# A streaming trunk's first norm: x in a second layout, squares summed by ScalarE's accumulator, the scale spread by a matmul

## The chip, the cores and the metric

The kernel runs on one core of a Trainium2 chip. The metric is the time of one execution on the device in microseconds (us). Before the change, three runs gave a median of 1671.03 us (1669.79 to 1671.99).

The engines of the core are called PE (TensorE, matrix products), ACT (ScalarE), DVE (VectorE), POOL (GpSimd) and SP (SyncE, which here only issues DMAs). PEld is PE's loading of stationary operands.

## The reference, cut to what matters

One layer of a trunk on x with 256 tokens and 2048 channels, all in float32. In short:

```python
h = rmsnorm(x, g1)                       # x * rsqrt(mean(x*x, channels) + 1e-6) * g1
xa, ya, cb, cc, cx, ga, gb = split(h @ w_in + b_in, 7)      # each 2048 wide
a = rg_lru(causal_conv4(xa) + bias)      # gates from lru_wr, lru_wi; a scan over tokens
out_a = (a * gelu(ya)) @ w_pa
out_b = (cb * causal_conv3(cc * cx)) @ w_pb
x = x + (sigmoid(ga) * out_a + sigmoid(gb) * out_b) @ w_o
x = x + relu(rmsnorm(x, g2) @ w_mlp1) ** 2 @ w_mlp2
out = rmsnorm(x, final_g)
```

## The kernel before, in words

All activations lie transposed: channels on the 128 partitions, tokens along the row. x is a tile of 128 x 16 x 256 (channel block k, token). A product takes weight blocks of 128 x 128 as the stationary operand and 256 tokens as the moving one.

To keep float32 accuracy on a faster matmul format, every operand is split into a high and a low part: ACT casts it to float32r (the high part, L51 for weights, L122 and L126 for activations), and DVE subtracts that from the original (the low part, L52, L123, L127). A block then takes two matmuls: L236 (L265 in the first four products) multiplies the high weight with both parts of the activation, 512 columns, and L237 (L266) the low weight with the high part, 256 columns. The two halves of the PSUM tile are added when it is evicted: `added` copies the second half to SBUF on ACT (L242) and adds the first on DVE (L244).

Weights come as slabs of 512 KB, eight blocks each (class `Weights`). A slab is loaded by SP (L59) into one of four raw buffers, then split into one of four buffers each for high and low parts. `take` asks for slabs up to three ahead of the one used (LOOK). The splits carry a higher priority than what stands around them in the program.

The first norm is folded: the products run on x * g1 without the scale rsqrt(mean + eps), and each evicted column block of `h @ w_in` is multiplied with the scale `rs` (L249) before the bias and the function are applied (L250). `rs` is a tile of 128 x 256, the same row on each partition. So the first products can start before the scale is known.

The start of the kernel, in the order in which the program is written:

1. Nine matmuls on a tile of ones (L161).
2. Eight times: a load of two channel blocks of x (256 KB, L164), the loads of w_in for those blocks (two of 256 KB, L179) and the splits.
3. Three slabs ahead (L185), then the rest of the parameters (L186; the first 16 columns came at L166).
4. `first_four`: four products of w_in at once, two of xa and two of ya, block by block as they land (L265, L266). They hold four PSUM buffers of the pool `psz`, which has six.
5. `first_norm`: eight squares on ACT (L274, 512 columns each), seven adds on DVE that fold them to two (L278), two matmuls with ones that sum over the partitions (L143), and `rsqrt`: square root on ACT (L150), then four arithmetic operations on DVE and a reciprocal, 256 columns each (L152 to L156).
6. Eight groups g of two column blocks. Group 0 begins with the evictions of the first four products (L293 and L301, through `z_done`), then runs the products cb, cc and cx; `decay` (L203, small operations on 128 x 16) stands in group 0 too. Then come the gates, the scan and the splits of the results.

Behind this come the merge, the output product, the two MLP stages and the final norm, none of which the diff touches.

The framework takes the program and writes one fixed list of instructions for each engine, and adds the semaphore waits that the data need. An engine's list is not always the order of the program: an instruction with a higher priority, or one whose inputs are expected earlier, can stand ahead. On the chip each engine works through its list in order and waits where an instruction's inputs or buffers are not there.

Of the kernel before, what the change touches and what calls it, by code (L numbers as in the profile page):

```python
# [9 lines left out]
F32 = mybir.dt.float32  # L10
F32R = mybir.dt.float32r
AF = mybir.ActivationFunctionType
ALU = mybir.AluOpType
# [12 lines left out]
WAKE = 9  # L26

PARAMS = [("g1", NT), ("g2", NT), ("gf", NT), ("b_in", 7 * NT), ("ca_w", 4 * NT), ("ca_b", NT),
          ("br", NT), ("bi", NT), ("lam", NT), ("cb_w", 3 * NT), ("one", 1)]
OFF = {}  # L30
_n = 0
for _name, _w in PARAMS:
# [40 lines left out]


@with_exitstack
def trunk(ctx: ExitStack, tc: tile.TileContext, xT, par, w_in, w_lru, w_pa, w_pb, w_o, w_1, w_2, out):
    nc = tc.nc
    big = ctx.enter_context(tc.tile_pool(name="big", bufs=3))
    keep = ctx.enter_context(tc.tile_pool(name="keep", bufs=1))
# [37 lines left out]
    def pc(name, j):  # L117
        return pr[:, OFF[name] + j:OFF[name] + j + 1]
# [55 lines left out]
    for i in range(NT // 2):  # L174
        load_x(2 * i, 2)
        c, o = divmod(i, HALF // 2)
        raw = rawp.tile([P, 4, 2 * P], F32, name="raw")
        for q, z in enumerate((Z_XA, Z_YA)):
            nc.sync.dma_start(raw[:, 2 * q:2 * q + 2, :],  # L179
                              w_in[z:z + 2, c, :, o * 2 * P:(o + 1) * 2 * P].rearrange("m p n -> p m n"))  # L180
            if i == 0:
                W.split(fhi[:, i, 2 * q:2 * q + 2], flo[:, i, 2 * q:2 * q + 2], raw[:, 2 * q:2 * q + 2])
        if i:
            W.split(fhi[:, i], flo[:, i], raw)
    W.ahead(LOOK)  # L185
    nc.sync.dma_start(pr[:, NT:], par[:, NT:])  # L186

    def squares(src, j):

# [57 lines left out]
    def z_done(ps, j, dst, func):  # L247
        t = added(ps)
        nc.vector.tensor_tensor(t, t, rs, ALU.mult)  # L249
        nc.scalar.activation(dst, t, func, bias=pc("b_in", j))  # L250

    def z_product():
        return product(lambda k: xg[:, k], 0, 2)

    def z_tile(j, dst, func):
        z_done(z_product(), j, dst, func)
# [11 lines left out]

    early = first_four()

    def first_norm(pool):
        parts = [pool.tile([P, 2, S], F32, name=n) for n in ("xc", "gy", "cb", "cc", "gate0", "gate1", "q", "v")]
        for k in range(HALF):
            nc.scalar.activation(parts[k], x[:, 2 * k:2 * k + 2, :], AF.Square, scale=pc("one", 0))  # L274
        n = HALF // 2
        while n:
            for k in range(n):
                nc.vector.tensor_tensor(parts[k], parts[k], parts[n + k], ALU.add)  # L278
            n //= 2
        rsqrt(rs, [parts[0][:, 0, :], parts[0][:, 1, :]])  # L280

    ua = big.tile([P, NT, 2, S], F32R, name="big")
    ub = big.tile([P, NT, 2, S], F32R, name="big")
    with tc.tile_pool(name="w1", bufs=1) as w1:
        first_norm(w1)
        for g in range(NB):
            xa = w1.tile([P, 2, S + 3], F32, name="xa")
            xc = w1.tile([P, 2, S], F32, name="xc")
# [1 line left out]
            for m in range(2):  # L290
                j = 2 * g + m
                nc.gpsimd.memset(xa[:, m, 0:3], 0.0)
                z_done(early[m] if g == 0 else z_product(), Z_XA + j, xa[:, m, 3:], AF.Identity)  # L293
                c = xc[:, m, :]
                nc.vector.tensor_scalar(c, xa[:, m, 3:], pc("ca_w", 3 * NT + j), pc("ca_b", j), ALU.mult, ALU.add)
                for tap in (2, 1, 0):
                    nc.vector.scalar_tensor_tensor(c, xa[:, m, tap:tap + S], pc("ca_w", tap * NT + j), c, ALU.mult, ALU.add)  # L297
                split(xs[:, m], c)
            gy = w1.tile([P, 2, S], F32, name="gy")
            for m in range(2):  # L300
                z_done(early[2 + m] if g == 0 else z_product(), Z_YA + 2 * g + m, gy[:, m, :], AF.Gelu_apprx_tanh)  # L301
            cb = w1.tile([P, 2, S], F32, name="cb")
            cc = w1.tile([P, 2, S], F32, name="cc")
            cx = w1.tile([P, 2, S + 2], F32, name="cx")
# [147 lines left out]
```

## Time and profile before

| | |
|---|---|
| median of three runs | 1671.03 us |
| time of the profiled execution | 1670.37 us |
| its span, first to last instruction | 1668.5 us |
| PE busy | 1648.3 us, 99% |
| DVE busy | 1124.8 us, 67% |
| ACT busy | 866.2 us, 52% |
| mean granted clock of PE | 0.996 |

The profile is of one execution. Times in timelines count from the span's start. Busy time of PE is modelled from pipelined matmuls, so consecutive matmuls overlap in the rows: the pace is read from the distance of their starts. The granted clock is a share of full speed. "idle before <-X" says how long the engine was idle before an instruction, and which instruction's end released it.

### The profile page before, as it was taken

The numbers are of one execution on the slowest core, as the hardware profiler recorded it, in microseconds if no ns is written. First come the engines' busy times: TensorE is split into PE (matmuls) and PEld (weight loads), VectorE is DVE, ScalarE is ACT, GpSimd is POOL, SyncE is SP. The second block draws the span as 40 slices with busy tenths as digits, with TensorE's granted clock in tenths as the row PEclk, the third lists the DMA queues.
The fourth block names the chain that finished last, engine by engine and source line by source line (L and its number), as shares of the span: only waits on it lengthen the run. The fifth ranks groups of instructions, "written<-read, shape, count | busy, mean of one in ns | idle before, by whom it ended". The sixth has DMA issues, their size and how long they took to land.

```text
span 1668.5 us, 24306 instructions
## 1 busy us (share of the span) xinstructions
PE 1648.3 (99%) x9468; PEld 1440.4 (86%) x9468; DVE 1124.8 (67%) x1606; ACT 866.2 (52%) x1259; POOL 3.4 (0%) x37
## 2 busy tenths in 40 slices
PE   9899999999999999999999999999999999999996
PEld 8788888888888888888888888888888888888886
DVE  6889778878977565666666766665555666655554
ACT  7666656666665444444455544444443444444442
POOL 0000000000000000000000000000000000000000
PEclk9999999999999999999999999999999999999998
DMA  8455555555556555555555555555555555555552
GB/s 282 152 190 189 190 187 187 183 190 189 188 181 196 189 186 187 188 188 189 190 189 184 183 190 189 188 189 187 187 187 188 188 189 189 189 189 188 188 186 96
DMA packets 89715, 312.14 MB, mean 187 GB/s; under 512 B 9856, under 2 KB 14336, under 8 KB 89600
## 3 DMA queue, kind: packets, MB, share of 16 engines
q1 hardware_dynamic: 89312, 309.93, 56.2%
q8 instruction: 74, 1.21, 0.3%
q10 hardware_dynamic: 288, 0.66, 0.1%
q14 instruction: 41, 0.34, 0.1%
HBM read 308.45 MB, written 2.10 MB: 186 GB/s over the span
## 4 chain that ended last, share of the span: by engine, by line
PE 98%; DVE 1%; DMA 0%; ACT 0%; issue 0%; DVEq 0%; SPq 0%
PE psz L236 63%; PE psz L237 32%; PE psz L265 1%; PE psz L266 0%; PE psl L330 0%; PE psl L331 0%; PE psl L329 0%; DVE wlo L52 0%; PE psz L233 0%; PE psz L234 0%; PE psz L232 0%; DVE x L406 0%; DMA raw<-w_in_s 0%; DVE t L153 0%; DVE v L351 0%
## 5 line engine op out<-in xcount | busy, mean ns | idle before, releaser
L236 PE MATMUL psz<-big,whi 128*128 128x512 f32 x4016 | 1409.5, 394 | 4.8 <-DVE t L244 4.6
L237 PE MATMUL psz<-big,wlo 128*128 128x256 f32 x4016 | 1121.5, 279 | 0.0
L52 DVE TENSOR_TENSOR wlo<-raw,whi 128x1024 fp32r<-128x1024 f32 x576 | 703.6, 1224 | 509.0 <-ACT whi L51 507.8
L51 ACT CAST whi<-raw 128x1024 fp32r<-128x1024 f32 x576 | 604.5, 1049 | 767.4 <-issue 432.2
L236 PEld LDWEIGHTS psz<-big,whi 128*128 128x128 f32 x4016 | 753.3, 188 | 185.1 <-issue 4.9
L237 PEld LDWEIGHTS psz<-big,wlo 128*128 128x128 f32 x4016 | 753.3, 188 | 0.0
L236 PE MATMUL psz<-mg,whi 128*128 128x512 f32 x496 | 174.6, 395 | 0.0
L237 PE MATMUL psz<-mg,wlo 128*128 128x256 f32 x496 | 139.0, 281 | 0.0
L236 PEld LDWEIGHTS psz<-mg,whi 128*128 128x128 f32 x496 | 93.0, 187 | 22.1 <-DVE mg L123 0.3
L244 DVE TENSOR_TENSOR t<-psz,low 128x256 f32<-128x256 f32 x255 | 105.9, 418 | 0.0
L242 ACT COPY low<-psz 128x256 f32<-128x256 f32 x255 | 93.1, 365 | 3.1 <-DVE t L244 2.7
L237 PEld LDWEIGHTS psz<-mg,wlo 128*128 128x128 f32 x496 | 93.7, 189 | 0.0
L249 DVE TENSOR_TENSOR t<-t,rs 128x256 f32<-128x256 f32 x112 | 47.4, 424 | 2.3
L383 DVE SCALAR_TENSOR_TENSOR s<-t 128x256 f32<-128x256 f32 x64 | 27.2, 426 | 2.1
L341 DVE RECIPROCAL q<-q 128x512 f32<-128x512 f32 x8 | 26.8, 3348 | 0.0
L265 PE MATMUL psz<-big 128*128 128x512 f32 x64 | 23.5, 424 | 0.6 <-ACT big L51 0.6
L297 DVE SCALAR_TENSOR_TENSOR xc<-xa,pr,xc 128x256 f32<-128x256 f32 x48 | 22.2, 485 | 0.0
L123 DVE TENSOR_TENSOR big<-s,big 128x256 fp32r<-128x256 f32 x48 | 20.1, 419 | 0.0
L122 ACT CAST big<-s 128x256 fp32r<-128x256 f32 x48 | 19.3, 402 | 0.0
L330 PE MATMUL psl<-xs,whi 128*128 128x256 f32 x64 | 18.0, 281 | 0.0
L331 PE MATMUL psl<-xs,wlo 128*128 128x256 f32 x64 | 17.9, 280 | 0.0
L329 PE MATMUL psl<-xs,whi 128*128 128x256 f32 x64 | 17.8, 278 | 0.0
(126 smaller groups left out, 575.0 us busy)
## 6 DMA issues: line engine op xcount, KB each, us to landing
raw<-w_s SPq DMA_DIRECT2D x256, 512.0 KB, 3.7
raw<-w_in_s SPq DMA_DIRECT2D x216, 512.0 KB, 4.0
raw<-w_pb_s SPq DMA_DIRECT2D x32, 512.0 KB, 4.3
raw<-w_pa_s SPq DMA_DIRECT2D x32, 512.0 KB, 4.3
raw<-w_o_s SPq DMA_DIRECT2D x32, 512.0 KB, 3.5
raw<-w_in_s SPq DMA_DIRECT2D x16, 256.0 KB, 5.8
raw<-w_lru_s SPq DMA_DIRECT2D x8, 512.0 KB, 3.5
x<-xT SPq DMA_DIRECT2D x8, 256.0 KB, 5.8
```

Source lines behind the costliest of these rows:

```text
L51: self.nc.scalar.copy(hi, raw)
L52: self.nc.vector.tensor_tensor(lo, raw, hi.bitcast(F32), ALU.subtract)
L123: nc.vector.tensor_tensor(dst[:, 1, :], src, dst[:, 0, :].bitcast(F32), ALU.subtract)
L236: nc.tensor.matmul(ps, hi[:, k * P:(k + 1) * P], a, start=i == 0, stop=False)
L237: nc.tensor.matmul(ps[:, 1, :], lo[:, k * P:(k + 1) * P], a[:, 0, :], start=False, stop=i == n - 1)
L242: nc.scalar.copy(low, ps[:, 1, :])
L244: nc.vector.tensor_tensor(t, ps[:, 0, :], low, ALU.add)
L249: nc.vector.tensor_tensor(t, t, rs, ALU.mult)
L265: nc.tensor.matmul(four[m], hi, xg[:, k], start=k == 0, stop=False)
L297: nc.vector.scalar_tensor_tensor(c, xa[:, m, tap:tap + S], pc("ca_w", tap * NT + j), c, ALU.mult, ALU.add)
L341: nc.vector.reciprocal(q, q)
L383: nc.vector.scalar_tensor_tensor(v, t, 0.0, t, ALU.max, ALU.mult)
```

## The change

x is passed in a second time as `xt`, with tokens on the partitions: 2 halves of 128 tokens x 2048 channels. Behind the loop of step 2, eight pieces of 128 x 512 (256 KB each) are loaded by SP into the tiles that later serve group 0, and ACT squares each in place while its accumulator writes the sum of each row to one column of `acc` (128 x 2 x 4). The rest of the parameters is loaded behind them, and the three slabs (`W.ahead(LOOK)`) behind that. The parameters get an identity matrix, 128 columns, in the place of one column of ones.

`first_norm` then works on 128 x 2 values: a sum over the four columns, mean and eps, square root on ACT, a reciprocal and three operations of a correction step on DVE. To bring the scale from the partitions to the row, each half is multiplied into the identity matrix and a matmul with ones sums over the partitions (128 columns each). ACT copies the result from PSUM to `rs`.

The evictions of the first four products are written inside `tc.issue_after(scaled)`: whatever this block puts on the engine of `scaled` (ACT, the copy to `rs`) is listed behind that copy on the engine.

```diff
+    places = ExitStack()
+    w1 = places.enter_context(tc.tile_pool(name="w1", bufs=1))
+    acc = keep.tile([P, 2, 4], F32, name="acc")
+    for i, n in enumerate(("xc", "gy", "cb", "cc", "gate0", "gate1", "q", "v")):
+        h, q = divmod(i, 4)
+        part = w1.tile([P, 2, S], F32, name=n)
+        nc.sync.dma_start(part, xt[h, :, q * 512:(q + 1) * 512])
+        nc.scalar.activation(part, part, AF.Square, accum_out=acc[:, h, q:q + 1])
+    nc.sync.dma_start(pr[:, NT:], par[:, NT:])
     W.ahead(LOOK)
-    nc.sync.dma_start(pr[:, NT:], par[:, NT:])
...
-    def first_norm(pool):
-        parts = [pool.tile([P, 2, S], F32, name=n) for n in ("xc", "gy", "cb", "cc", "gate0", "gate1", "q", "v")]
-        for k in range(HALF):
-            nc.scalar.activation(parts[k], x[:, 2 * k:2 * k + 2, :], AF.Square, scale=pc("one", 0))
-        n = HALF // 2
-        while n:
-            for k in range(n):
-                nc.vector.tensor_tensor(parts[k], parts[k], parts[n + k], ALU.add)
-            n //= 2
-        rsqrt(rs, [parts[0][:, 0, :], parts[0][:, 1, :]])
+    def first_norm():
+
+        r = keep.tile([P, 2], F32, name="r")
+        y = keep.tile([P, 2], F32, name="y")
+        m = keep.tile([P, 2], F32, name="m")
+        nc.vector.tensor_reduce(r, acc, mybir.AxisListType.X, ALU.add)
+        nc.vector.tensor_scalar(r, r, 1.0 / D, EPS, ALU.mult, ALU.add)
+        nc.scalar.activation(y, r, AF.Sqrt)
+        nc.vector.reciprocal(y, y)
+        nc.vector.tensor_tensor(m, r, y, ALU.mult)
+        nc.vector.scalar_tensor_tensor(m, m, -0.5, y, ALU.mult, ALU.mult)
+        nc.vector.scalar_tensor_tensor(m, m, 1.5, y, ALU.add, ALU.mult)
+        ps = psl.tile([P, 512], F32, name="psl")
+        eye = pr[:, OFF["eye"]:OFF["eye"] + P]
+        for h in range(2):
+            d = wk.tile([P, S], F32, name="s")
+            nc.vector.tensor_scalar(d[:, :P], eye, m[:, h:h + 1], None, ALU.mult)
+            nc.tensor.matmul(ps[:, h * P:(h + 1) * P], ones, d[:, :P], start=True, stop=True)
+        return nc.scalar.copy(rs, ps[:, :S]).ins
...
-    with tc.tile_pool(name="w1", bufs=1) as w1:
-        first_norm(w1)
+    with places:
+        scaled = first_norm()
+        def z_early(m, j, dst, func):
+            with tc.issue_after(scaled):
+                z_done(early[m], j, dst, func)
+
...
-                z_done(early[m] if g == 0 else z_product(), Z_XA + j, xa[:, m, 3:], AF.Identity)
+                if g == 0:
+                    z_early(m, Z_XA + j, xa[:, m, 3:], AF.Identity)
+                else:
+                    z_tile(Z_XA + j, xa[:, m, 3:], AF.Identity)
...
-                z_done(early[2 + m] if g == 0 else z_product(), Z_YA + 2 * g + m, gy[:, m, :], AF.Gelu_apprx_tanh)
+                if g == 0:
+                    z_early(2 + m, Z_YA + m, gy[:, m, :], AF.Gelu_apprx_tanh)
+                else:
+                    z_tile(Z_YA + 2 * g + m, gy[:, m, :], AF.Gelu_apprx_tanh)
```

## Rows read from the trace of the kernel before

**Rows 1.** The page's part 1, PE's busy time with its share of the span, and the first line of part 4, the chain that ended last by engine.

```profile
PE 1648.3 (99%) x9468; PEld 1440.4 (86%) x9468; DVE 1124.8 (67%) x1606; ACT 866.2 (52%) x1259; POOL 3.4 (0%) x37
...
PE 98%; DVE 1%; DMA 0%; ACT 0%; issue 0%; DVEq 0%; SPq 0%
```

**Rows 2.** The longest of PE's waits from 60 us to the end: engine, line, what it waited for, us in total, times, longest.

```profile
PE psl L143 <- ACT s L400: 1.0, 1, 1.0
```

**Rows 3.** The table of stages: from and to in us, length, busy time of each engine with its number of instructions, granted clock of PE, mean busy share of the DMA engines, GB/s.

```profile
5.75:30.50 24.75, 24.75 (x128) 21.25 (x129) 19.70 (x27) 19.75 (x30) 0.00 (x0) 1.00 1.02 339
30.50:41.70 11.20, 11.20 (x66) 9.65 (x64) 8.37 (x11) 7.79 (x12) 0.00 (x0) 1.00 0.60 214
41.70:47.65 5.95, 1.31 (x7) 0.71 (x5) 5.51 (x16) 3.45 (x6) 0.00 (x0) 1.00 0.57 176
47.65:51.38 3.73, 3.73 (x13) 3.21 (x13) 3.73 (x13) 2.17 (x6) 0.00 (x0) 0.54 0.02 4
51.38:70.00 18.62, 18.62 (x109) 16.26 (x108) 15.48 (x37) 12.43 (x20) 0.14 (x2) 1.00 0.42 145
```

**Rows 4.** The timeline of PE: start, duration, engine, line, operation, out<-in, shape, count, idle time before. The first row is the first product, the others lie around its long idle time.

```profile
5.75 0.80 PE L265 MATMUL psz<-big 128*128 128x512 f32 x1 [0.56 <-ACT big L51]
...
41.59 0.28 PE L237 MATMUL psz<-big,wlo 128*128 128x256 f32 x1
41.96 1.13 PE L143 MATMUL psl<-xc,ones 128*128 128x256 f32 x4
47.65 0.77 PE L236 MATMUL psz<-big,whi 128*128 128x512 f32 x1 [4.55 <-DVE t L244]
...
51.38 0.39 PE L236 MATMUL psz<-big,whi 128*128 128x512 f32 x1
```

**Rows 5.** The timeline of ACT in the same stretch.

```profile
41.79 1.04 ACT L51 CAST whi<-raw 128x1024 fp32r<-128x1024 f32 x1 [1.75 <-PE psz L236]
42.85 1.28 ACT L150 ACT_TABLE_LOAD   x1
44.15 0.47 ACT L150 ACTIVATE t<-psl,eps 128x256 f32<-128x256 f32 x1
44.52 0.64 ACT L242 COPY low<-psz 128x256 f32<-128x256 f32 x2
```

**Rows 6.** The timeline of DVE in the same stretch.

```profile
41.22 0.69 DVE L278 TENSOR_TENSOR xc<-xc,gy 128x512 f32<-128x512 f32 x1
...
45.48 1.74 DVE L153 RECIPROCAL t<-t 128x256 f32<-128x256 f32 x1
47.14 0.36 DVE L244 TENSOR_TENSOR t<-psz,low 128x256 f32<-128x256 f32 x1
```

**Rows 7.** Groups of instructions by line and shape from 0 to 60 us: line, engine, operation, out<-in, shapes, count, then busy us in total, mean ns of one, idle us before them.

```profile
L52 DVE TENSOR_TENSOR wlo<-raw,whi 128x1024 fp32r<-128x1024 f32 x11 | 13.5, 1224 | 4.2 <-ACT whi L51 3.9
...
L51 ACT CAST big<-raw 128x512 fp32r<-128x512 f32 x2 | 1.2, 618 | 1.1 <-DMA raw<-w_in_s 1.1
...
L214 DVE TENSOR_SCALAR sd<-sd 128x16 f32<-128x16 f32 x5 | 0.9, 171 | 0.1
...
L274 ACT ACTIVATE gy<-x,pr 128x512 f32<-128x512 f32 x1 | 0.7, 710 | 0.0
...
L152 DVE TENSOR_SCALAR low<-psl 128x256 f32<-128x256 f32 x1 | 0.4, 418 | 0.0
...
L208 DVE RECIPROCAL sd<-sd 128x16 f32<-128x16 f32 x1 | 0.3, 253 | 0.0
```

**Rows 8.** The timeline of SP's queue: start, time to issue, line, what is loaded, count.

```profile
14.97 0.34 SPq L164 DMA_DIRECT2D x<-xT  x1
15.92 0.88 SPq L179 DMA_DIRECT2D raw<-w_in_s  x2
18.11 4.69 SPq L59 DMA_DIRECT2D raw<-w_in_s  x3
22.85 0.43 SPq L186 DMA_DIRECT2D pr<-par  x1
```

**Rows 9.** The timeline of ACT from 20 us: casts of the last two pieces of the first four products (big), casts of the slabs (whi), and a cast and a square later on.

```profile
20.14 1.05 ACT L51 CAST big<-raw 128x1024 fp32r<-128x1024 f32 x1 [0.32 <-DMA raw<-w_in_s]
...
22.25 1.05 ACT L51 CAST big<-raw 128x1024 fp32r<-128x1024 f32 x1 [0.25 <-DMA raw<-w_in_s]
23.51 1.05 ACT L51 CAST whi<-raw 128x1024 fp32r<-128x1024 f32 x1 [0.21 <-DMA raw<-w_in_s]
24.84 1.05 ACT L51 CAST whi<-raw 128x1024 fp32r<-128x1024 f32 x1 [0.28 <-DMA raw<-w_in_s]
...
33.39 1.05 ACT L51 CAST whi<-raw 128x1024 fp32r<-128x1024 f32 x1 [1.62 <-PE psz L236]
34.35 0.72 ACT L274 ACTIVATE gate<-x,pr 128x512 f32<-128x512 f32 x1
```

**Rows 10.** The timeline of PE where the product after the first four begins.

```profile
30.50 0.40 PE L236 MATMUL psz<-big,whi 128*128 128x512 f32 x1
30.74 0.28 PE L237 MATMUL psz<-big,wlo 128*128 128x256 f32 x1
30.86 0.39 PE L236 MATMUL psz<-big,whi 128*128 128x512 f32 x1
```

**Rows 11.** DMA issues: what is loaded, queue, count, KB each, median us from issue to landing.

```profile
pr<-par SPq DMA_DIRECT2D x1, 160.5 KB, 3.7
```

More of the change, by code (lines that the diff above doesn't have):

```diff
@@ L28 @@
 PARAMS = [("g1", NT), ("g2", NT), ("gf", NT), ("b_in", 7 * NT), ("ca_w", 4 * NT), ("ca_b", NT),
-          ("br", NT), ("bi", NT), ("lam", NT), ("cb_w", 3 * NT), ("one", 1)]
+          ("br", NT), ("bi", NT), ("lam", NT), ("cb_w", 3 * NT), ("eye", P)]
 OFF = {}
@@ L75, in trunk @@
 @with_exitstack
-def trunk(ctx: ExitStack, tc: tile.TileContext, xT, par, w_in, w_lru, w_pa, w_pb, w_o, w_1, w_2, out):
+def trunk(ctx: ExitStack, tc: tile.TileContext, xT, xt, par, w_in, w_lru, w_pa, w_pb, w_o, w_1, w_2, out):
     nc = tc.nc
@@ L433 @@
         "xT": np.ascontiguousarray(x[0].T.reshape(NT, P, S).transpose(1, 0, 2)),
+        "xt": np.ascontiguousarray(x[0].reshape(2, P, D)),
         "par": np.ascontiguousarray(np.concatenate([_cols(v) for v in (
-            norm1_g, norm2_g, final_g, b_in, conv_a_w, conv_a_b, lru_br, lru_bi, lru_lam, conv_b_w, np.ones(P, np.float32))], 1)),
+            norm1_g, norm2_g, final_g, b_in, conv_a_w, conv_a_b, lru_br, lru_bi, lru_lam, conv_b_w, np.eye(P, dtype=np.float32))], 1)),
         "w_in_s": _slabs(np.asarray(w_in)[0]),
```

## The prediction

> **What bounds the kernel now.** I read the page's busy shares and its chain of waits first, then a table of stages, then the timelines of single engines around the one stage that differs.
>
> TensorE (PE) is busy 99% of the span, and the chain that ends last is 98% PE [rows 1]. A change elsewhere counts only where it makes PE wait or frees it from a wait. After 60 us its longest wait is 1.0 us, on a line at the kernel's end that isn't touched [rows 2]. So whatever is gained or lost before 60 us arrives at the end unchanged: the rest runs behind PE at a fixed pace.
>
> The table of stages shows where PE is not full. From 5.75, the first product, to 41.70 it is full at clock 1.00; from 41.70 to 47.65 it works 1.31 of 5.95 us; from 47.65 to 51.38 it is busy, but at a granted clock of 0.54, between its two levels of 1.2 and 2.4 GHz (0.5 and 1.0); from 51.38 it is back at 1.00 [rows 3].
>
> PE's timeline names the wait. The last product matmul starts at 41.59, four small matmuls of the scale (L143) run at 41.96, then there are 4.55 us of idleness that end with L244 on VectorE (DVE) [rows 4]. L244 is the eviction of one of the first four products. Their four PSUM buffers and the two of the next two products fill the pool of six, so the seventh product must wait for an eviction, although the first four products were complete by 30.50, where the product after them starts [rows 10].
>
> Why was the eviction late? On ScalarE (ACT) the copies L242 come right behind the square root L150 (44.15), which comes behind a table load (42.85) and the matmuls of the scale; these wait for the last of seven adds L278 at 41.22 on DVE [rows 4 to 6]. DVE then gives 1.74 us to the reciprocal of 256 columns before it does L244 at 47.14 [rows 6]. The path is: squares, tree of adds, L143, L150, L153, L244, PE.
>
> **What the change takes away.** Without the wait the seventh product would begin at about 41.70 instead of 47.65, which is 5.95 us. Six pairs of matmuls (L236 with L237) then took 51.38 - 47.65 = 3.73 us; at the pitch of the pairs before the wait, 0.35 us (from the pair of 30.50 to that of 30.86, which I round down) [rows 4, 10], they take 2.10 us. So the low clock cost 1.63 us. The prize is 5.95 + 1.63 = 7.58 us.
>
> DVE loses seven adds (7 x 0.69 = 4.8 us) and five operations on 256 columns, a reciprocal of 1.74 and four like L152 of 0.42 (3.4 us) [rows 6, 7]. It gets six operations on at most 8 columns; the nearest rows are those on 16 columns, 0.17 us and 0.25 us for the reciprocal [rows 7], about 1.1 us. Two products with eye have 128 columns, between the 0.17 of 16 columns and the 0.42 of 256: I take 0.30 each. Net, DVE gets about 6.6 us of room in a stage where it was busy 5.51 of 5.95 us [rows 3]. It needs that room, since it now has 7.6 us less in which to do the same splits and evictions.
>
> ACT keeps eight squares of 512 columns. They were 0.71 to 0.72 each; no row shows the accumulator, so the bounds are 0.62 (the cast of 512 columns, without an operand from SBUF for the scale) and 0.96 (0.71 and a small operation of 0.25 behind it) [rows 7]. I take 0.85, between the same function on the same shape and the upper end. The square root was 0.47 on 256 columns; on two it is at least the 0.17 of the smallest rows, and I take 0.2 [rows 5, 7]. A copy of the scale out of PSUM comes in, between half of the two L242 of 0.64, 0.32, and the 0.47 of L150: 0.4 [rows 5].
>
> **What it adds.** (a) Two matmuls of 128 columns instead of two of 256. Before, two calls gave four instructions in 1.13 us [rows 4]. Half the columns bound it from below, 0.57, the same from above: I take 0.7 on PE.
>
> (b) Eight loads of 256 KB and a longer parameter row, ahead of the weight slabs in SP's queue. SP keeps the written order: x of 14.97, the two halves of 15.92, three slabs from 18.11, and only then the parameters at 22.85, though those waited for nothing [rows 8]. So the new loads follow the halves of 15.92 and delay nothing of the first four products. They do delay the slabs. One round of x and the two halves, 768 KB, lands each 2.11 us (casts that wait for it begin at 20.14 and 22.25), at a DMA share of 1.02 [rows 3, 9]. That is 0.70 us per 256 KB, 5.6 us for eight; two slabs of 512 KB land 1.33 us apart (23.51, 24.84), 0.67 per 256 KB, 5.3 us [rows 9]. I take 5.6, as x is the row with the same size and shape. The parameters move ahead too: 321 columns were 160.5 KB [rows 11]; with 127 columns more they are 224 KB, 0.6 us at the same rate. SP's own issuing, eight like the 0.34 of x at 14.97 [rows 8], is 2.7 us and shorter than the transfers.
>
> The first slab then lands at 23.51 + 6.2 = 29.7. Its cast takes 1.05 and its low part 1.22 [rows 7, 9]: high part at 30.8, low part at 32.0. PE wants the high part at 30.50 and the low one 0.24 later [rows 10]: a wait of 0.3 and then one of 1.0, together 1.3 us. Later slabs land each 1.33 us and PE needs 8 x 0.35 = 2.8 for one, so there is no second wait. The cover that hid the loads was the lead of the first slab, and it is spent once.
>
> (c) The chain of the scale. The last half landed at 22.25, so x in the second layout is complete at about 27.9 and summed at 28.8 [rows 9]. Table load 1.28 [rows 5], square root 0.2, four small DVE operations with their handovers about 0.9, two products with eye 0.6: 31.8 for the operand of the second matmul. If the low part of the first slab gets in between on DVE, it is 33.0; if the table load and the square root go ahead of that slab's cast, the low part comes at 32.6 instead of 32.0.
>
> (d) The new wait: the ACT part of the first evictions may not go ahead of the copy of the scale. Queued behind it are the casts of later slabs, the evictions and the activations. It hurts only if the matmuls of the scale stand late in PE's order. At about 33 us it is 8 us before the seventh product wants a buffer.
>
> (b) and (c) fall on PE at the same place, between the first four products and the next. If the matmuls of the scale stand exactly there, PE waits until 31.8 to 33.0 (1.3 to 2.5 us); if they stand later, it waits 1.3 for the slab alone. I take 2.0 us, in the upper half, since both chains use the same two engines. Sum: 7.58 - 0.7 - 2.0 = 4.9 us. The profiled execution took 1670.37 us for a span of 1668.5, so 1665.5 in its terms. The median of the three runs lies 0.66 higher, at 1671.03: 1666.1, which I round to 1666.0. With the wait anywhere from 0.8 to 3.2 us, its own range is 1664.9 to 1667.3.
>
> One price has two sources. The row shows a table load of 1.28 us with nothing around it: the cast before it ends at 42.83, it starts at 42.85, and the square root starts at 44.15 [rows 5]. The Trainium skill (ScalarE: Activation LUTs, "What ACT_TABLE_LOAD costs") adds a drain of about 1.38 us to the load, 2.66 us per switch. By that page the chain would end 1.4 us later and, if PE waits for it, the time would be about 1667.4; the trace of this kernel shows no such gap, so the sum goes by the row.
>
> **The rivals.**
> *The clock falls again* (14%). The new wait is about 2 us. After the 4.55 us of idleness the clock was 0.54; a gap of 0.56 us before the first product left it at 1.00 [rows 3, 4]; nothing lies between. If it falls, another 1.63 us go: gain 3.3 us, 1667.7. For it: the two waits, slab and scale, may add up. Against: PE works in between them.
>
> *The scale goes late* (10%). In the kernel before, the scale's matmuls stood behind both following products. If they still do, PE reaches them at 41.70 + 1.3 = 43.0, then 0.7 for them, 0.4 for the copy of the scale, 0.32 for L242 and 0.36 for L244 [rows 5, 6]: PE goes on at 44.8, as the evictions had to wait on ACT. Against 47.65 + 1.63 that gains 4.5 us, 1666.5. Against: the operand was ready only at 41.9 then, now near 32.
>
> *The scale goes too early: slower* (12%). PE takes its instructions in a fixed order. If the scale's matmuls stand inside the first four products, at a place that PE reaches at p, PE waits from p to 31.8 and the rest of the products behind it. Price: (31.8 - p) + 0.7 + 1.63 for the clock, against 7.58; it is slower than before from p below 26.5, and by 0.2% (3.3 us) from p below 23.2. At p = 22 the change is +4.6 us: 1675.6. For it: ACT held ready squares back behind a cast that waited for PE until 33.39 [rows 9], so the fixed order does misjudge who is ready. Against: the loads stand behind all that the first four products need.
>
> *No change* (6%): the first evictions are early, but DVE, with 7.6 us less time, is late with splits and PE loses the same 7 us in the next products: about 1671. For it: DVE is busy 15.48 of 18.62 us even after the wait [rows 3]. Against: 6.6 us less work.
>
> **Chances.** 58% for the forecast. 0.2%, 3.3 us, is about what a measurement of this kernel can tell from no change, so faster means under 1667.7. The forecast gives 54 faster and 4 same, the clock 7 and 7, the late scale 7 and 3, the early scale 2 same and 10 slower, no change 4 same and 2 slower: faster 0.68, same 0.20, slower 0.12. The range goes down to 1663.8 (nearly no wait for the slab: 7.58 - 0.6 from 1671.03 is 1664.1) and up to 1671.0, which leaves out the slower case and part of no change.
>
> **What would show it.** Right: the idleness at 41.96 to 47.65 gone, the clock 1.00 throughout, L242 of the first four at 32 to 36, the first slab's cast near 30, a wait of 1 to 3 us on PE near 31. Wrong: matmuls of the scale among those of L265, a low clock after 31, casts that wait behind the copy of the scale, or a new PE wait for wlo after 35.

## The result, and the profile after

The changed kernel took 1661.86 us, the median of four runs (1660.12 to 1663.2); beside them the kernel before took 1670.6 (four runs, 1669.79 to 1671.99). The ratio is 0.9946, 95% interval 0.9929 to 0.9963. The forecast was 1666.0 with a range from 1663.8: the direction was right, the gain of 8.7 us is nearly twice the 4.9 forecast, and the time lies below the range. The experiments show that most of this gain has nothing to do with the norm: with the operands at the distance that they have in the kernel before, the change is worth 2.4 us.

The profiled execution took 1660.12 us for a span of 1658.2, 10.3 less than before. Part 1 of the page and the head of its chain, which answer to [rows 1]:

```profile
PE 1639.7 (99%) x9468; PEld 1435.1 (87%) x9468; DVE 1118.4 (67%) x1602; ACT 865.7 (52%) x1268; POOL 3.4 (0%) x37
...
PE 97%; DMA 1%; DVE 1%; ACT 1%; SPq 0%; issue 0%; DVEq 0%
```

PE has the same 9468 matmuls and is busy 8.6 us less. That can't be a removed wait, since a wait is not busy time; and a stretch at a low clock, which makes work longer, is in both kernels ([rows 3] and the stages below) and was worth only 1.63 us before. So most of it must be matmuls that follow each other faster.

**The start.** The stages of the kernel after, columns as in [rows 3]:

```profile
5.37:30.25 24.88, 24.07 (x128) 19.44 (x128) 15.82 (x25) 20.62 (x41) 0.00 (x0) 1.00 1.05 366
30.25:34.66 4.41, 1.93 (x8) 1.12 (x6) 4.06 (x22) 3.48 (x6) 0.00 (x0) 0.80 0.43 172
34.66:38.07 3.41, 3.41 (x15) 3.01 (x16) 3.41 (x7) 3.29 (x7) 0.00 (x0) 0.75 0.64 202
38.07:70.00 31.93, 31.93 (x191) 28.35 (x190) 26.01 (x51) 19.82 (x30) 0.14 (x2) 1.00 0.69 214
```

The idle time at 41.70 is gone, and PE is full from 34.66 on. In its place stands a stage from 30.25 in which PE works 1.93 of 4.41 us, and a low clock in it and in the next stage. PE's timeline there (it answers to [rows 4, 10]):

```profile
30.14 0.28 PE L275 MATMUL psz<-big 128*128 128x256 f32 x1
32.79 0.70 PE L245 MATMUL psz<-big,whi 128*128 128x512 f32 x1 [2.38 <-ACT whi L51]
33.33 1.22 PE L297 MATMUL psl<-s,ones 128*128 128x128 f32 x4
34.66 0.58 PE L246 MATMUL psz<-big,wlo 128*128 128x256 f32 x1
```

PE waits 2.38 us for the high part of the first slab and then works slowly; the granted clock is 0.50 from 34.66 to 36.32 and 0.99 from there to 38.07. From 30.25 to 38.07 PE starts eight pairs, which need 8 x 0.35 = 2.8 us, so the place cost 5.0 us, where the forecast had 2.0 + 0.7 = 2.7. Of it, 32.79 - 30.25 = 2.5 is the wait, and the 5.28 us from 32.79 on hold 2.8 of pairs, 0.7 of the scale's matmuls (their length at full clock in a run below) and 1.8 more. The low clock did not take all of that. The matmul at 34.66 needs the low part of the slab, and DVE's timeline shows when that was made:

```profile
33.38 1.22 DVE L52 TENSOR_TENSOR wlo<-raw,whi 128x1024 fp32r<-128x1024 f32 x1
```

It was ready at 34.60. At full clock PE would have been through with the scale's matmuls near 33.7 (32.79 + 0.24 + 0.7, an estimate), so about 0.9 us is a second wait, for the low part, which the slow matmuls hide. The rest, 0.8 us, is the low clock behind 34.66: 3.41 us for what takes 0.12 + 7 x 0.35 at full clock. ACT's timeline says why the slab was late (it answers to [rows 5, 9]):

```profile
27.93 0.63 ACT L193 ACTIVATE v<-v 128x512 f32<-128x512 f32 x1
28.47 0.19 ACT L193 ACTIVATION_READ_ACCUMULATOR v<-v 128x1 f32 x1
28.56 0.20 ACT L214 ACTIVATE s<-pr 128x16 f32<-128x16 f32 x1
28.78 1.28 ACT L215 ACT_TABLE_LOAD   x1
30.07 0.22 ACT L215 ACTIVATE sg<-s 128x16 f32<-128x16 f32 x1
30.31 1.28 ACT L287 ACT_TABLE_LOAD   x1
31.60 0.20 ACT L287 ACTIVATE y<-r 128x2 f32<-128x2 f32 x1
31.71 1.98 ACT L51 CAST whi<-raw 128x1024 fp32r<-128x1024 f32 x2
34.59 0.37 ACT L298 COPY rs<-psl 128x256 f32<-128x256 f32 x1 [0.90 <-PE psl L297]
```

The cast at 31.71 has no idle time before it: the slab had landed, and ACT was busy. Ahead of it stand not one table load but two. L214 and L215 are `decay`, the small piece of group 0; it took the place between the last square and the square root, and its sigmoid needs another table than the root. That is 30.31 - 28.56 = 1.75 us in front of both the scale and the slab. Up to the squares all went as forecast; the queue of SP (it answers to [rows 8]):

```profile
17.29 0.34 SPq L192 DMA_DIRECT2D xc<-xt  x1
...
23.35 0.43 SPq L194 DMA_DIRECT2D pr<-par  x1
23.88 2.38 SPq L59 DMA_DIRECT2D raw<-w_in_s  x4
```

**The rest.** Each group's first gate matmul is a mark in PE's order. All its 64 executions, with the first and last start; before, then after:

```profile
L329 PE MATMUL psl<-xs,whi x64: 277/278/281, 71.7 to 485.9; 128*128 128x256 f32 x64
```

```profile
L357 PE MATMUL psl<-xs,whi x64: 280/281/283, 68.6 to 479.2; 128*128 128x256 f32 x64
```

At the first mark the changed kernel is 3.1 us ahead, at the last 6.7. Of the 3.1, the start explains 7.58 - 5.0 = 2.6, and the first four products, complete at 30.25 instead of 30.50, another 0.25. Between the marks PE had no long wait to lose [rows 2]; the matmuls themselves come faster. The starts of the 512-column matmuls (L236, L245) in three stretches, one for the groups, one for the merge, one for the MLP; the number in brackets is the count. Before:

```profile
100.00:450.00 350.00, 333.30 (x953) 1.00 0.57 188
600.00:800.00 200.00, 200.00 (x572) 1.00 0.57 189
1000.00:1500.00 500.00, 500.00 (x1430) 1.00 0.57 188
```

After:

```profile
100.00:450.00 350.00, 333.30 (x962) 1.00 0.58 190
600.00:800.00 200.00, 200.00 (x567) 1.00 0.56 186
1000.00:1500.00 500.00, 500.00 (x1444) 1.00 0.58 190
```

The clock is 1.00 in all six rows. A pair of matmuls took 500 / 1430 = 349.7 ns before and 346.3 after in the MLP, but 200 / 572 = 349.7 and 352.7 in the merge. Read from the starts of single pairs, the kernel before runs at 350.0 ns nearly everywhere, the kernel after at 346.7 or at 353.3. With 4512 such pairs, 3.3 ns on each is 15 us. In this execution the groups gained 6.7 - 3.1 = 3.6 us; the first product of the MLP is at a lead of 3.6 again (one pair, by its number in the order, starts at 943.37 before and 939.77 after), so the merge and the output product lost 3.1; and the MLP gained the remaining 6.7 of the 10.3.

And the pace can change within a stream, at a wait. The kernel after at 502 us, PE's timeline:

```profile
501.70 0.39 PE L245 MATMUL psz<-big,whi 128*128 128x512 f32 x1
501.93 0.28 PE L246 MATMUL psz<-big,wlo 128*128 128x256 f32 x1
502.04 0.39 PE L245 MATMUL psz<-big,whi 128*128 128x512 f32 x1
...
502.91 0.50 PE L245 MATMUL psz<-big,whi 128*128 128x512 f32 x1 [0.36 <-DVE big L123]
...
504.08 0.40 PE L245 MATMUL psz<-big,whi 128*128 128x512 f32 x1
504.31 0.28 PE L246 MATMUL psz<-big,wlo 128*128 128x256 f32 x1
504.43 0.40 PE L245 MATMUL psz<-big,whi 128*128 128x512 f32 x1
```

From 501.70 to 502.04 the next pair follows after 0.34 us, from 504.08 to 504.43 after 0.35; over more rows that is 346.7 ns ahead of the wait and 353.3 behind it, on the same line with the same tiles.

What differs in the products between the two kernels? Not an instruction. But 127 more columns of parameters and four small tiles lie ahead of the weight buffers in SBUF, 608 bytes on each partition. The compiled programs give these addresses (not a view of the profile):

```
                       before     after
big  (moving)           16512     16512
whi  (stationary)      151840    152448
mg   (moving)          193824    194432
whi - big, mod 256        160         0
whi - mg,  mod 256          0         0
```

In what follows "distance" is that of `big`, the moving tile of the weight products. Two places read `mg` instead: the output product, and one half of each of the last 16 products of the MLP. The three `big` buffers and the four `whi` buffers each lie a multiple of 256 apart, so it is one number for a kernel.

### The profile page after: what moved, and what is told of

Its sections match the earlier page's. It is cut to its first block, busy times and chain, and to the rows that moved or that the text cites. A ratio compares the mean times of both kernels' runs of the same rounds, so it can differ in the third digit from the quotient of the medians.

```text
span 1658.2 us, 24317 instructions
## 1 busy us (share of the span) xinstructions
PE 1639.7 (99%) x9468; PEld 1435.1 (87%) x9468; DVE 1118.4 (67%) x1602; ACT 865.7 (52%) x1268; POOL 3.4 (0%) x37
## 4 chain that ended last, share of the span: by engine, by line
PE 97%; DMA 1%; DVE 1%; ACT 1%; SPq 0%; issue 0%; DVEq 0%
PE psz L245 63%; PE psz L246 32%; DMA raw<-w_in_s 1%; PE psl L357 0%; PE psl L358 0%; PE psl L359 0%; DMA x<-xT 0%; DVE wlo L52 0%; PE psz L243 0%; PE psz L242 0%; PE psz L241 0%; DVE x L434 0%; SPq L179 0%; DVE t L153 0%; ACT gate L193 0%
## 5 line engine op out<-in xcount | busy, mean ns | idle before, releaser
L245 PE MATMUL psz<-big,whi 128*128 128x512 f32 x4016 | 1401.4, 395 | 2.7 <-ACT whi L51 2.4
L245 PEld LDWEIGHTS psz<-big,whi 128*128 128x128 f32 x4016 | 753.6, 188 | 178.0 <-ACT whi L51 2.7
L245 PE MATMUL psz<-mg,whi 128*128 128x512 f32 x496 | 174.5, 397 | 0.0
L245 PEld LDWEIGHTS psz<-mg,whi 128*128 128x128 f32 x496 | 93.2, 188 | 22.7 <-DVE mg L123 0.2
L251 ACT COPY low<-psz 128x256 f32<-128x256 f32 x255 | 92.8, 365 | 0.0
```

Of the source, the lines that this page charges most:

```text
L245: nc.tensor.matmul(ps, hi[:, k * P:(k + 1) * P], a, start=i == 0, stop=False)
L251: nc.scalar.copy(low, ps[:, 1, :])
```

## The experiments

**First set: is the pace in the run, in the work or in the addresses?** a1 and a2 are the two kernels unchanged, once more. a3 is the kernel before with the 608 bytes and none of the new work; a4 is the changed kernel with 32 bytes more.

> The kernel before, unchanged, profiled a second time. Theory (phase): PE's matmul pairs run at one of a few fixed paces (346.7, 350.0, 353.3 ns a pair), and which one is settled anew each time PE restarts after a wait; with the same waits the paces of the first profile come back: 350.0 in the group stage, in the merge and in the MLP, 353.3 only from the output product's wait near 851 us to that near 941 us; span 1668 to 1671 us. Rival (run by run): the pace is chance of the single run, and this profile shows other paces in the same stages, with a span that may differ by 5 us or more.

> The changed kernel, unchanged, profiled a second time. Theory (phase): again 346.7 ns a pair in the group stage, 353.3 in the merge, 346.7 in the MLP, with at most one stage on another pace (its four timed runs spread over 3 us, which is a third of what one stage's pace is worth), span 1658 to 1662. Rival (run by run): the stages have other paces than in the first profile.

```diff
 # a3, on the kernel before
-          ("lam", NT), ("cb_w", 3 * NT), ("one", 1)]
+          ("lam", NT), ("cb_w", 3 * NT), ("one", 1), ("pad", P - 1)]
...
+    for n in ("p0", "p1", "p2", "p3"):
+        pad = keep.tile([P, 2], F32, name=n)
+        nc.vector.memset(pad, 0.0)
```

> The kernel before with all buffers behind the parameters at the addresses of the changed kernel (the parameter row is 127 columns wider, four small tiles are added); the work and its order are the same. Rival (addresses): the pace comes with the addresses of the weight buffers, so the group stage and the MLP run at 346.7 ns a pair and the merge at 353.3: about 7 us faster than before, 1663 to 1665 us. Theory (phase): the waits of the kernel before are all there, so the paces stay at 350.0 and the time at 1669 to 1672, unless the longer parameter load shifts a wait; then single stages change by 3.3 ns a pair, in either direction.

```diff
 # a4, on the kernel after
     ssq = keep.tile([P, S], F32, name="ssq")
+    pad = keep.tile([P, 2], F32, name="p0")
+    nc.vector.memset(pad, 0.0)
```

> The changed kernel with all buffers behind the parameters 32 bytes further on, so that the weight buffers lie 32 bytes off a multiple of 64 as they do in the kernel before. Rival (addresses): the paces of the kernel before come back (350.0 ns a pair nearly everywhere): 1667 to 1668 us, the gain at the start of 2.9 us alone. Theory (phase): 1660 to 1664 us with the same paces as the changed kernel.

a1 took 1671.3 us with its old paces. a2 took 1656.12, and this time the merge too ran at 346.7. So on `big` the kernel before has one pace, and the kernel after chooses between two. a3 took 1663.5 (five runs, 1656.09 to 1664.74), ratio 0.9948 [0.993, 0.9967]: the old work with the new addresses gains what the whole change gains. a3, the same windows and its first gate:

```profile
100.00:450.00 350.00, 333.29 (x960) 1.00 0.58 189
...
1000.00:1500.00 500.00, 500.00 (x1443) 1.00 0.59 190
```

```profile
L332 PE MATMUL psl<-xs,whi x64: 277/281/283, 71.6 to 483.2; 128*128 128x256 f32 x64
```

The counts are those of the kernel after, and the first gate at 71.6 is that of the kernel before: the start of a3 gained nothing, all its gain is pace. a4 shows the other sign: 32 bytes turn the change into a loss, 1676.99 us, ratio 1.0034 [1.0021, 1.0047], with its first gate at 71.1, paces that alternate from group to group, and 353.3 in the merge and the MLP. Neither of its two forecasts had that.

**Second set: what made the start late?** b1 lists `decay` behind the copy of the scale; b2 takes the order off the evictions; b3 loads the slabs ahead of the second layout; b4 is b1 and b3 together. All four have the distance 0, so their pace is 346.7 or 353.3 as it falls out, and what they tell of the start is read at the first gate.

```diff
 # b1
             if g == 0:
-                decay()
+                with tc.issue_after(scaled):
+                    decay()
```

> The changed kernel with the ScalarE work of decay listed behind the copy of the scale, so that its table load and its sigmoid no longer stand between the last square and the square root and the first slab's cast. What counts is the start of group 0's gate matmuls (71.7 and 72.6 us in the two profiles of before, 68.6 and 71.0 in those of the change). Theory (the new wait was mis-sized because decay's 1.7 us and a second table load stand ahead of the square root and of the cast of the first slab): the cast goes from 31.7 to about 30.0, PE's wait behind the first four products falls from 2.5 us to 1 us or less, and the gates begin 1.5 to 3.5 us earlier than with the change, at 66 to 68. Rival (the slab's landing behind the new loads sets the wait): the cast waits for the DMA instead, PE waits as long, gates at 68.5 to 71.

b1 took 1649.67 us, first gate 66.2. PE and ACT of b1, each a timeline:

```profile
31.73 0.71 PE L297 MATMUL psl<-s,ones 128*128 128x128 f32 x4 [1.11 <-DVE s L296]
32.20 0.47 PE L245 MATMUL psz<-big,whi 128*128 128x512 f32 x1
33.06 0.39 PE L246 MATMUL psz<-big,wlo 128*128 128x256 f32 x1 [0.39 <-DVE wlo L52]
```

```profile
29.07 1.28 ACT L287 ACT_TABLE_LOAD   x1
30.37 0.20 ACT L287 ACTIVATE y<-r 128x2 f32<-128x2 f32 x1
30.48 1.03 ACT L51 CAST whi<-raw 128x1024 fp32r<-128x1024 f32 x1
```

One table load is left ahead of the cast, PE waits 1.11 and 0.39 us instead of 2.5, and the four matmuls of the scale take 0.71. The clock doesn't fall. 28 to 46 us, after and b1, columns as in the stages:

```profile
28.00:46.00 18.00, 15.52 (x80) 12.96 (x79) 15.04 (x40) 13.63 (x23) 0.00 (x0) 0.91 0.75 256
```

```profile
28.00:46.00 18.00, 16.50 (x95) 14.11 (x94) 14.90 (x31) 15.76 (x28) 0.00 (x0) 1.00 0.76 269
```

Fifteen matmuls more in the same stretch, at 1.00 instead of 0.91. So `decay` ahead of the root cost the change 2.4 us at the first gate of these two executions. That is the low end: the other three executions with the change's order (a2, a4, c4) have their first gates at 71.0, 71.1 and 70.0, with mean clocks of 0.81, 0.81 and 0.91 from 28 to 46 us, and a second execution of b1's program (d4) has it at 65.4.

```diff
 # b2
         def z_early(m, j, dst, func):
-            with tc.issue_after(scaled):
-                z_done(early[m], j, dst, func)
+            z_done(early[m], j, dst, func)
```

> The changed kernel without the order of the first evictions behind the copy of the scale. The framework then lists two to three of the evictions' copies ahead of the table load of the square root and of the first slab's cast. Theory (ScalarE's list ahead of the first slab's cast sets PE's wait): the cast comes 0.5 to 1 us later, and so do PE and the gates: 69 to 72. Rival (the order of evictions costs what it makes wait): the evictions come at 29 to 31 instead of 34.9, nothing else changes, gates at 67 to 68.

b2 took 1658.77 us, first gate 73.7, later than in the kernel before and later than either forecast. Its longest PE wait and ACT's timeline:

```profile
PE psl L297 <- DVE s L296: 4.0, 1, 4.0
```

```profile
29.46 0.37 ACT L251 COPY low<-psz 128x256 f32<-128x256 f32 x1 [2.00 <-PE psz L275]
29.73 0.64 ACT L193 ACTIVATE q<-q 128x512 f32<-128x512 f32 x1
```

An eviction of the first four products stands on ACT ahead of the last two squares and waits 2.00 us for PE; the squares, the root and the slab's cast wait behind it. So the order that the change puts on the evictions is not a cost but a part of its gain, 3 to 5 us at the first gate (73.7 in this one execution against 71.0 in a2 and 68.6), and b2's total hides that, since its pace was 346.7 in the groups, the merge and the MLP.

```diff
 # b3 (b4: this and b1's edit)
     acc = keep.tile([P, 2, 4], F32, name="acc")
+    W.ahead(LOOK)
     for i, n in enumerate(("xc", "gy", "cb", "cc", "gate0", "gate1", "q", "v")):
...
     nc.sync.dma_start(pr[:, NT:], par[:, NT:])
-    W.ahead(LOOK)
```

> The changed kernel with the three slabs loaded ahead of x's second layout instead of behind it. Theory (the lead of the slabs is what the new loads cost): the first slab is cast near 23.5 as before the change, PE runs through without a wait near 30.5 and without a low clock, and the gates begin 6 to 7.5 us earlier than in the kernel before, at 64.5 to 66. Rival (the scale's chain sets the wait): x lands 4 us later, the scale's matmuls wait for it and PE with them, gates at 68 or later. For the time, the start gives 3 to 5 us against the change, if the pace of the later stages is that of the change: 1657 to 1660; a stage on another pace moves it by 3 to 7 us.

> The changed kernel with both: three slabs ahead of x's second layout, and decay's ScalarE work behind the copy of the scale. Theory: as with the slabs first, gates at 64.5 to 66; decay is off the chain, so the scale is ready 1.7 us earlier, which PE doesn't need. Rival (scale's chain): earlier than with the slabs first alone, by up to 1.7 us. Time 1657 to 1660 if the later stages keep the pace of the change.

b3 took 1657.96 (1651.43 to 1659.17), ratio 0.9914 [0.9889, 0.9939], b4 1653.2 (1648.93 to 1659.5), below the expected 1657 to 1660, ratio 0.9897 [0.987, 0.9925]. Both have their first gate at 65.5. b4's row shows the place closed:

```profile
28.00:46.00 18.00, 18.00 (x105) 15.66 (x104) 9.93 (x22) 15.54 (x34) 0.00 (x0) 1.00 0.83 305
```

PE is busy all 18 us. Given the slabs first, the order of `decay` doesn't move the first gate; it spares PE a wait of 0.6 us for the first low part, in an execution whose first four products ended 0.4 us later. b4 has the lowest median of the kernels that were timed several times and beats both kernels; its interval overlaps that of b3, and at its distance the time also depends on the paces that a run falls into.

**Third set: size of the shift, its place, or the distance?** c1 and c2 give the kernel before 96 and 128 unused bytes ahead of the weights, for distances of 0 and 32. c3 puts the 608 bytes behind the weights: distance 160 as before, and all that lies behind moved. c4 gives the kernel after 416 bytes, so that it has the old distance of 160.

```diff
 # c1, c2 on the kernel before (24 and 32 columns); c4 on the kernel after (104 columns)
+    pad = keep.tile([P, 24], F32, name="p0")
+    nc.vector.memset(pad, 0.0)
...
 # c3, on the kernel before, between the pools lop and wk
+    gap = ctx.enter_context(tc.tile_pool(name="gap", bufs=1))
+    pad = gap.tile([P, 152], F32, name="p0")
+    nc.vector.memset(pad, 0.0)
```

> The kernel before with one unused tile of 96 bytes, so that the weight buffers start at a multiple of 128 bytes; nothing else. Theory (addresses): the pair pace is that of the other kernels whose weight buffers start at a multiple of 128, 346.7 or 353.3 ns in each stage and never 350.0; with 346.7 in the group stage and the MLP the time is 1656 to 1665 us, at the same start as before (gates at 71.6 to 72.6 us). Rival (not this alignment, but the larger shift, the wider parameter row or its longer load): 350.0 as before, 1669 to 1672.

> The kernel before with one unused tile of 128 bytes: the weight buffers keep their place within 128 bytes (32 past a multiple) and change it within 256 (from 32 to 160, as in the changed kernel moved by 32 bytes). Theory (place within 128 bytes): 350.0 ns a pair as before, 1669 to 1672 us. Rival (place within 256 bytes): 346.7 and 353.3 in alternation, as in the changed kernel moved by 32 bytes, 1665 to 1677.

> The kernel before with what lies behind the weight buffers (the small work tiles, group tiles and mg) moved by 608 bytes, the weight buffers left where they are. Theory (the weights' addresses set the pace): 350.0 ns in the group stage, merge and MLP, 1668 to 1672 us; only the output product, which reads mg, may change. Rival (the other tiles' addresses): 346.7 or 353.3 as in the kernel whose buffers were all moved by 608 bytes.

> The changed kernel with one unused tile of 416 bytes, so that its weight buffers have the place within 256 bytes (and 1024) that they have in the kernel before. Theory (the weights' addresses set the pace): 350.0 ns a pair nearly everywhere, so that the change's own worth is left: gates 1 to 3 us earlier than in the kernel before and the end as much, 1667.5 to 1670 us. Rival (the pace is not of the addresses but of the work and its waits): 346.7 and 353.3 as in the changed kernel, 1656 to 1664 us.

c1 took 1678.5 us: a miss on the time, since its merge and MLP settled at 353.3; it kept to 346.7 in most groups and never showed 350.0. c2 took 1678.83, a little above what was expected, with the alternating paces of a4, which has the same distance of 32 and other work. c3 took 1672.22 at 350.0, its first gate being late at 73.9 (its first product began at 7.00). Its output product, which reads another moving tile, `mg`, ran at 350.0 as well, where it runs at 353.3 in the kernel before: only c3 moves `mg` against the weights, from the distance 0 to 160. The 512-column matmuls of the output product from 860 to 930 us, before and c3:

```profile
860.00:930.00 70.00, 70.00 (x199) 1.00 0.57 188
```

```profile
860.00:930.00 70.00, 70.00 (x201) 1.00 0.57 188
```

The kernel before shows the same within single products. In the last ones of the MLP, where one half of the pairs reads `mg` and the other `big`, with the same weight buffers, the first take 347.3 ns (distance 0) and the second 350.4 (160), means over 15 products (a1 and c4 repeat this within 0.1). So it is the distance of the two operands of a matmul that counts, not an address by itself.

c4 is the comparison that the change deserves. At the distance of the kernel before:

```profile
100.00:450.00 350.00, 333.30 (x953) 1.00 0.58 188
...
1000.00:1500.00 500.00, 500.00 (x1430) 1.00 0.59 188
```

The counts are those of the kernel before. c4 took 1668.72 us (ten runs, 1667.16 to 1670.19) beside 1671.16, ratio 0.9985 [0.9976, 0.9995]. The change itself is worth 2.4 us (0.8 to 4.0 by the interval). With the pace equal, start and end agree: in c4's profile the place costs 5.9 us (from 30.53 to 38.50, less six pairs), which leaves 7.58 - 5.9 = 1.7, and this execution took 1.65 us less than the profiled one of the kernel before.

**Fourth set: has each distance its own pace?** d1, d2 and d3 are b4 with 64, 128 and 192 bytes ahead of the weights, which are also their distances. d4 is b1 again, timed in several runs.

```diff
 # d1, on b4 (d2: 32 columns, d3: 48)
+    pad = keep.tile([P, 16], F32, name="p0")
+    nc.vector.memset(pad, 0.0)
```

> The changed kernel with the slabs first and decay behind the scale (1653 us in its timed runs, between 1649 and 1660), and one unused tile of 64 bytes. With it the distance from the moving operand to the weight buffers is 64 bytes within 256 (0 in the changed kernel, 160 in the kernel before). Theory (distance within 256 bytes sets the paces open to PE): away from 0 and 32 there is one steady pace; at 64 it is either still the pair 346.7 and 353.3, or 350.0 all through, then 1659 to 1662 us with a spread of 3 us or less. Rival (the distance of 160 is a single case): 346.7 and 353.3 with a spread of 8 us or more, 1649 to 1668.

> The same with a tile of 128 bytes: distance 128. Theory: 350.0 ns a pair in group stage, merge and MLP, as at 160, 1659 to 1662 us with a spread of 3 us or less. Rival: 346.7 and 353.3, spread of 8 us or more.

> The same with a tile of 192 bytes: distance 192. Theory: 350.0 ns a pair as at 160, 1659 to 1662 us with a spread of 3 us or less. Rival: 346.7 and 353.3, spread of 8 us or more.

> The changed kernel with decay's ScalarE work behind the copy of the scale, now timed. Theory: the start of its first profile comes back (gates at 66 to 67 us), but its pace of 346.7 ns in every stage was one of several: the runs spread from 1649 to 1662 us as those with the slabs first do, with a median of 1650 to 1658. Rival (this program always settles at 346.7): all runs between 1648 and 1651.

d1 took 1675.19 (1674.78 to 1676.84), d2 1667.01 (1666.13 to 1668.28), d3 1676.85 (1676.23 to 1677.27), with first gates at 64.8, 65.5 and 64.9. The paces and times were a miss in all three, where 350.0, or at 64 perhaps 346.7 and 353.3, with 1659 to 1662 us was expected: d2 runs at 351.1, d1 and d3 at 353.3 in the groups, the merge and the MLP. That each has one steady pace there, with runs that lie within 2.2 us of each other, held. The output product, whose `mg` is at distance 0 in all three, goes its own way: 346.9 in d1, 346.8 in d2, 352.9 in d3. d1's row, to be read beside the two of 860 to 930 us above:

```profile
860.00:930.00 70.00, 70.00 (x203) 1.00 0.59 189
```

d4 took 1658.16 (1656.97 to 1659.03), ratio 0.9923 [0.9908, 0.9937]: b1's single 1649.67 was one outcome of several, though the four runs spread less and lie a little higher than was expected. All together, for the products on `big`:

| distance | kernels | ns per pair | us (medians, or the one run) |
|---|---|---|---|
| 0 | after, a2, a3, b1 to b4, c1, d4 | 346.7 or 353.3, settled anew at some waits | 1649.67 to 1678.5 |
| 32 | a4, c2 | 346.7 and 353.3 by turns, then 353.3 | 1676.99, 1678.83 |
| 64 | d1 | 353.3 | 1675.19 |
| 128 | d2 | 351.1 | 1667.01 |
| 160 | before, a1, c3, c4 | 350.0 | 1668.72 to 1672.22 |
| 192 | d3 | 353.3 | 1676.85 |

That the distance counts modulo 256 is supported from two sides: 32 and 160 are equal modulo 128 and have other paces, and c3's `mg` at 416 modulo 512 has the pace of `big` at 160.

## Why the prediction was wrong, step by step

*"So whatever is gained or lost before 60 us arrives at the end unchanged: the rest runs behind PE at a fixed pace."* This step failed, and it took the result out of the range. PE has no long wait there, but its pace is not fixed: a3 gains 7.5 us of pace with nothing changed in the start, and c4 leaves of the change 2.4 us once the pace is the old one. That the measured time moved the forecast way by this much is luck: 32 bytes more, and it moves the other way (a4). A busy share of 99% and equal instructions were read as equal time. The widened parameter row stood in the diff, and I priced its transfer only.

*"I take 2.0 us"* and the sum *"7.58 - 0.7 - 2.0 = 4.9 us"*: the wait for the high part measured 2.5, another 0.9 is the wait for the low part behind it, and the sum left the clock at 1.00, where the low clock took some 0.8 us more: 4.2 in the place of 2.0. The rival "the clock falls again", held at 14%, is what happened: 0.50 from 34.66 to 36.32 after a wait of 2.38 us, where in b1 a wait of 1.11 left it at 1.00. Its 1667.7 us is near c4's 1668.72, the measurement at the distance for which it was worked out, though it put less on the waits (2.0) and more on the clock (1.63). What carried the wait that far is an item that the chain (c) lacked: `decay` with its own table load, 1.75 us, listed ahead of the root and of the slab's cast. I asked what is queued behind the copy of the scale, and not what could come ahead of the root. In b1, with `decay` out of the way, the two waits of the forecast ("a wait of 0.3 and then one of 1.0", or 1.3 to 2.5 where the scale's matmuls stand there) come to 1.11 + 0.39 = 1.5.

What held. The prize of 7.58 us: b4, without any wait or low clock there, has its first gate 6.2 us before that of the kernel before, 6.8 when each is counted from the last matmul of its first four products (30.99 and 30.38), and 7.58 - 0.7 is 6.9. SP's order and the landing of the second layout: the last square ended at 28.56, forecast 28.8, although one square with the read of its accumulator takes 0.61 to 0.72 us from start to start (b2 and the kernel after) and not 0.85. The copy of 0.37 (forecast 0.4), the four matmuls of 0.71 at full clock (0.7) and DVE's relief of 6.4 us (1124.8 - 1118.4, forecast 6.6) were right. L251 began its evictions at 34.86, inside 32 to 36. No engine became the bound, and no wait for wlo came behind that of the first slab.

The table load: the Trainium skill (ScalarE: Activation LUTs, "What ACT_TABLE_LOAD costs") adds a drain of about 1.38 us to a load of 1.283. Both loads of the kernel after take 1.28 us and the next function starts 0.01 us behind each, so here the row was right and no drain is seen.

What stays open: why PE's pace depends on the distance of its operands, and what decides at a wait between 346.7 and 353.3; a3 and c1 have the same work and the same distance of 0, and c1's one run took 1678.5 where a3's five took 1656.09 to 1664.74. Only six distances were tried, four of them in one or two kernels, all on one kernel's pair of 512 and 256 columns.

## What to carry to other kernels

Where PE is full, compare the matmul counts of equal windows before crediting an edit with a gain: any tile that changes size can shift the weight buffers and move the time by more than the edit, so give both versions the same addresses and time them again. When a step moves on an engine, read the whole list in front of it, small operations that switch an activation table above all. And a wait added on purpose can be a gain, if it keeps an instruction that depends on a slow engine out of the way of ready work.

## What the runs showed of the hardware

In a dense stream of float32r matmuls at a granted clock of 1.00, a pair of 512 and 256 columns took 346.7, 350.0, 351.1 or 353.3 ns, by the distance modulo 256 bytes between the SBUF addresses of its stationary and its moving operand. The work of b4 took 1653.2 us at one distance and 1676.85 at another. At the distance 0 the pace is one of two and can change at a wait of 0.36 us, so that runs of one program spread by 10 us (b4); at 32 both paces occur as well (a4, c2). At 64, 128, 160 and 192 the runs of one program keep within 3.5 us. The effect goes by the pair of operands: in one execution, on the same weight buffers, `mg` at distance 0 ran at 346.9 and `big` at distance 64 at 353.3 (d1). The Trainium skill (SBUF — State Buffer, "Operand start alignment") asks for no more than a multiple of the element size and says that this is about legality and not about speed; these runs show 1.4% between two such addresses (1676.85 / 1653.2).

The accumulator of ACT is read by an instruction of its own, 0.19 us long, behind each square of 0.63.
